# Gate and up products taken for two weight tiles at a time in a decoder layer

## The chip, the cores and the metric

The kernel runs on one core of one Trainium2 chip. The metric is the device time of one execution in microseconds, as the median of several runs. One further execution was recorded by the hardware profiler; the engines are called PE (TensorE, the matmuls), PEld (its weight loads), DVE (VectorE), ACT (ScalarE), POOL (GpSimd) and SP (SyncE, which issues most DMAs).

## What is computed

One layer of a decoder on 256 tokens of 1024 features, in float32: a half feed-forward block, a token mixer, cross-attention to 256 memory tokens, and a second half feed-forward block. The change lies in the two feed-forward blocks:

```python
D_MODEL = 1024
SEQ = 256
D_FF = 2816

def swiglu(h, w_gate, w_up, w_down):
    return (jax.nn.silu(h @ w_gate) * (h @ w_up)) @ w_down

h = rmsnorm(x, ffn1_pre_g[l])
f = swiglu(h, ffn1_w_gate[l], ffn1_w_up[l], ffn1_w_down[l])
x = x + MACARON_WEIGHT * rmsnorm(f, ffn1_post_g[l])
...
h = rmsnorm(x, ffn2_pre_g[l])
f = swiglu(h, ffn2_w_gate[l], ffn2_w_up[l], ffn2_w_down[l])
x = x + MACARON_WEIGHT * rmsnorm(f, ffn2_post_g[l])
```

## The kernel before

**Numbers in two parts.** Matrix products run on operands in the reduced format fp32r. To keep float32's precision each operand is split into a high part (its value in fp32r) and a low part (the rest, in fp32r too), and a product is the sum of low x high, high x high and high x low. ScalarE makes the high part of a weight unit (L76), VectorE the low part (L77). The split of the activations stands in one tile `xs`: for each of the eight 128-feature chunks k, columns 0 to 255 are the high parts of the 256 tokens and columns 256 to 511 the low parts.

**Weights.** All weight tiles of 128 x 128 lie in memory in the order of their use, eight to a unit of 512 KB. `Weights.get` hands out the next tile as a pair (high, low). At the first tile of a unit it has SyncE's loads and the two splits made up to four units ahead; the buffers for high and low parts are six each, so a split waits until the matmuls of an older unit are done.

**Gate and up.** The hidden features are 22 tiles of 128. Features 0 and 1 go through another function (`group`). For each of the features 2 to 21, in each of the two blocks, `gate_up` makes two halves, s = 0 for gate and s = 1 for up. A half takes the eight tiles of one weight unit, k = 0 to 7, into one PSUM tile `ps` of 512 columns (`acc` for gate, `sm` for up in the profile). For every k there are two matmuls with the weights standing still and x moving: the low part of the weights with x's high part, 256 columns, into the right half of `ps` (L574, "short" below), and the high part of the weights with both parts of x, 512 columns, into all of `ps` (L575, "long" below). Each matmul loads its own 128 x 128 weights. At the end of a half ScalarE copies the right half out (L579) and VectorE adds the left half to it (L580). 20 features, 2 halves, 8 tiles and 2 blocks make 640 such pairs of matmuls.

**Around it.** Between the features stand the down products (`row_step`, L298 to L300): 12 matmuls of 512 columns for each feature, here with the activations standing still and the weights moving. Matmuls of 256 columns alone stand in the products of the mixer and the cross-attention (L173 to L175), matmuls of 512 columns alone in L260 to L262 and L298 to L300; the cross-attention's scores (L747 to L749) are twelve of 256 columns between two groups of twelve of 512.

**Order.** TensorE's order is the order in which the program is written, fixed by hand; the orders of the other engines are set by a scheduler, and by hand at the seams between the layer's parts.

Of the kernel before, what the change touches and what calls it, by code (L numbers as in the profile page):

```python
# [17 lines left out]
S = 256  # L18
ND = D // P
# [117 lines left out]
def build(nc, io, tiles_only=False):  # L137
    pr = Program()
    st = {}
# [7 lines left out]
    def tmp(shape, name, **kw):  # L147
        return st["tmp"].tile(shape, F32, name=name, **kw)
# [14 lines left out]
    def defer(run):  # L163
        st["w"].defer(run)
# [22 lines left out]
    def split_plain(X, k, src, eng=nc and nc.vector):  # L187
        nc.scalar.copy(X[:, k, :S], src)
        eng.tensor_tensor(X[:, k, S:], src, X[:, k, :S].bitcast(F32), op=ALU.subtract)
# [29 lines left out]
    def group(name, X, cols, done, before=None, hi_first=False):  # L219

        def run():
            ps = [accum() for _ in range(2)]
            o = [h for p in ps for h in halves(p)]

            def by_lo(ws, k, first):
                for i, (hi, lo) in enumerate(ws):
                    nc.tensor.matmul(o[i], lo, st[X][:, k, :S], start=first and i % 2 == 0,  # L227
                                     stop=k == ND - 1 and hi_first, skip_group_check=True)

            def by_hi(ws, k, first):  # L230
                for i, (hi, lo) in enumerate(ws):
                    nc.tensor.matmul(o[i], hi, st[X][:, k, :S], start=first and i % 2 == 0,  # L232
                                     stop=False, skip_group_check=True)
                    nc.tensor.matmul(o[i], hi, st[X][:, k, S:], start=False,  # L234
                                     stop=k == ND - 1 and not hi_first, skip_group_check=True)
            steps = (by_hi, by_lo) if hi_first else (by_lo, by_hi)
            for k in range(ND):
                if before:
                    before(k)
                ws = [st["w"].get() for _ in cols]  # L240
                for i, by in enumerate(steps):
                    by(ws, k, k == i == 0)
            done(ps)
        names = [name] * len(cols) if isinstance(name, str) else name
        pr.add(run, [(n, k * P, c) for k in range(ND) for n, c in zip(names, cols)])
# [61 lines left out]
    def row_step(X, k, first):  # L307
        w = st["w"].get(UNIT)
        for t in range(2):
            for d in HALVES:  # L310
                row_product(X, st["acc"], k, first, False, t, d, w)
# [47 lines left out]
    def x_spread():  # L359
        pb = rms_spread("x")  # L360
        rB = st["rBx"] = keep([P, S], "rBx")
        nc.scalar.copy(rB, pb[:, :S])
# [198 lines left out]
    def ffn(n, X, before, aside, last):  # L561
        wg, wu, wd = (f"ffn{n}_w_{s}" for s in ("gate", "up", "down"))

        def gate_up(f, done):

            box = []

            def half(s):
                def run():
                    ps = (accum, small)[s]()  # L570
                    for k in range(ND):
                        hi, lo = st["w"].get()
                        x = st[X][:, k, :]
                        nc.tensor.matmul(ps[:, S:], lo, x[:, :S], start=k == 0, stop=False, skip_group_check=True)  # L574
                        nc.tensor.matmul(ps, hi, x, start=False, stop=k == ND - 1, skip_group_check=True)  # L575
                    if s == 0:
                        box.append(st["ffn"].tile([P, 2, S], F32, name="gu", bufs=6))
                    c = tmp([P, S], "cmb")
                    nc.scalar.copy(c, ps[:, S:])  # L579
                    nc.vector.tensor_tensor(box[0][:, s, :], ps[:, :S], c, op=ALU.add)  # L580
                    if s:
                        done(box[0])
                return run
            return [(half(s), [(w, k * P, f * P) for k in range(ND)]) for s, w in enumerate((wg, wu))]

        def finish(f, t):

            src = t
            if f < 2:
                t = st["ffn"].tile([P, 2, S], F32, name="gu", bufs=6)  # L590
                src = src.rearrange("p (i s) -> p i s", i=2)
            nc.vector.tensor_tensor(t, src, st["rBx"][:, None, :].to_broadcast([P, 2, S]), op=ALU.mult)

            def rest():
                nc.scalar.activation(t[:, 0, :], t[:, 0, :], AF.Silu)
                nc.vector.tensor_tensor(t[:, 0, :], t[:, 0, :], t[:, 1, :], op=ALU.mult)
                h = st["h", f] = st["ffn"].tile([P, 1, 2 * S], F32R, name="h", bufs=LAG + 4)
                split_plain(h, 0, t[:, 0, :])
            defer(rest)

        early = []
        first = 2 if n == 1 else 3

        def opened():
            x_spread()
            for f, t in enumerate(early):
                finish(f, t)

        def down(k):
            if k == 0:  # L610
                pr.add(row_acc)
            pr.add(lambda: row_step(st["h", k], 0, k == 0), [(wd, k * P, c * P) for c in range(ND)])

        group([wg, wu] * 2, X, [0, 0, P, P], early.extend, before=before, hi_first=n == 1)
        seam(False)
        for f in range(2, NF):
            gate, up = gate_up(f, early.append if f < first + 1 else lambda t, f=f: finish(f, t))
            pr.add(*gate)
            if f == first:
                side(x_sums if n == 1 else x_root)  # L620
            if f == first + 1:
                side(opened)
            pr.add(*up)
            for run in aside.get(f, ()):
                pr.add(run)
            for k in {2: [], 3: [], 4: [], 5: [0], 6: [1, 2], 7: [3]}.get(f, [f - LAG]):
                down(k)
        down(NF - LATE - 1)
        ks = list(range(NF - LATE, NF))
        side(lambda: st["w"].defer(roots_next))  # L630
        return last(lambda k: st["h", k], ks, [(wd, k * P, c * P) for k in ks for c in range(ND)])
# [163 lines left out]
    def seam(on):  # L795
        pr.add(("seam", on))

    def side(func, *args):
        pr.add(lambda: func(*args))
# [138 lines left out]
    k = K.pop(0)  # L938
# [47 lines left out]
    k = K.pop(0)  # L986
# [141 lines left out]
```

## Time and profile before

| | before |
|---|---|
| median of 3 runs | 578.73 us |
| lowest to highest | 577.92 to 578.73 us |
| the profiled execution, its own time | 580.79 us |
| its span, first to last instruction | 578.6 us |
| PE busy | 565.5 us (98%) |
| PEld busy | 496.7 us (86%) |
| DVE busy | 411.2 us (71%) |
| ACT busy | 341.6 us (59%) |
| the 640 + 640 matmuls of L574 and L575, sum of their shown durations | 410.9 us |

The profile shows one execution. The end of a matmul is modelled and overlaps the next one's start, so the durations of matmuls add up to more than the time they take; the distance between two starts is the better measure. A weight load (PEld) runs beside the matmul ahead of it. The profile's times in order are rounded to 0.01 us, so a step is read over many matmuls, or from several of the same kind.

### The profile page before, as it was taken

How to read it: one execution, taken by the hardware profiler on the slowest of the kernel's cores; microseconds unless marked ns; L12 is line 12 of the kernel's file. 1: busy time of each engine (PE TensorE's matmuls, PEld its weight loads, DVE VectorE, ACT ScalarE, POOL GpSimd, SP SyncE). 2: the span in 40 equal slices, each digit the busy share in tenths (PEclk: the TensorE clock that was granted, in tenths of full speed). 3: DMA queues.
4: the chain of work that ended last, by engine and by line, in shares of the span. 5: the costliest groups of instructions: out<-in, count | busy, mean ns of one | idle time of the engine just before them, and what ended most of it. 6: DMA issues, size and time to landing. Idle time of an engine off the chain costs nothing.

```text
span 578.6 us, 8485 instructions
## 1 busy us (share of the span) xinstructions
PE 565.5 (98%) x3304; PEld 496.7 (86%) x3304; DVE 411.2 (71%) x662; ACT 341.6 (59%) x613; POOL 20.0 (3%) x37
## 2 busy tenths in 40 slices
PE   8799999999999999999999999999999999999995
PEld 8788888888888899988899988879888888888884
DVE  5898666787776678984568676467796766766654
ACT  6588575555555656775359456358674555555543
POOL 0000000000000000450000000001000000000001
PEclk9899999999999999999999999999999999999998
DMA  8885686645646068264256624426655555545202
GB/s 298 310 344 182 254 281 227 217 159 206 204 163 216 18 237 287 79 218 147 72 187 246 219 113 146 146 72 222 253 195 184 202 180 185 200 164 218 74 1 73
DMA packets 29400, 107.04 MB, mean 185 GB/s; under 512 B 2096, under 2 KB 3248, under 8 KB 28976
## 3 DMA queue, kind: packets, MB, share of 16 engines
q1 hardware_dynamic: 28928, 106.14, 52.3%
q8 instruction: 26, 0.43, 0.3%
q10 hardware_dynamic: 432, 0.35, 0.2%
q14 instruction: 14, 0.11, 0.0%
HBM read 105.44 MB, written 1.05 MB: 184 GB/s over the span
## 4 chain that ended last, share of the span: by engine, by line
PE 92%; DVE 3%; DMA 2%; ACT 1%; issue 1%; DVEq 0%; SPq 0%
PE acc L575 13%; PE sm L575 13%; PE acc L298 10%; PE acc L300 9%; PE acc L299 9%; PE acc L574 7%; PE sm L574 7%; PE acc L173 3%; PE acc L174 3%; PE acc L175 3%; PE acc L234 2%; PE acc L232 2%; PE acc L260 2%; PE acc L262 2%; PE acc L261 2%; PE acc L227 2%
## 5 line engine op out<-in xcount | busy, mean ns | idle before, releaser
L77 DVE TENSOR_TENSOR wlo<-wraw,whi 128x1024 fp32r<-128x1024 f32 x183 | 223.7, 1231 | 76.9 <-ACT whi L76 76.4
L76 ACT CAST whi<-wraw 128x1024 fp32r<-128x1024 f32 x184 | 192.5, 1053 | 51.1 <-PE acc L300 41.5
L575 PE MATMUL acc<-xs,whi 128*128 128x512 f32 x320 | 115.9, 401 | 0.0
L575 PE MATMUL sm<-xs,whi 128*128 128x512 f32 x320 | 114.5, 398 | 0.0
L574 PE MATMUL acc<-xs,wlo 128*128 128x256 f32 x320 | 90.4, 282 | 3.1 <-DVE wlo L77 3.1
L574 PE MATMUL sm<-xs,wlo 128*128 128x256 f32 x320 | 90.1, 282 | 0.0
L575 PEld LDWEIGHTS acc<-xs,whi 128*128 128x128 f32 x320 | 60.7, 190 | 14.6
L575 PEld LDWEIGHTS sm<-xs,whi 128*128 128x128 f32 x320 | 60.1, 188 | 14.9
L298 PE MATMUL acc<-whi,h 128*128 128x512 f32 x176 | 69.0, 392 | 0.0
L300 PE MATMUL acc<-whi,h 128*128 128x512 f32 x176 | 68.7, 390 | 0.0
L299 PE MATMUL acc<-wlo,h 128*128 128x512 f32 x176 | 68.5, 389 | 0.0
L574 PEld LDWEIGHTS acc<-xs,wlo 128*128 128x128 f32 x320 | 60.8, 190 | 4.5 <-DVE wlo L77 3.3
L574 PEld LDWEIGHTS sm<-xs,wlo 128*128 128x128 f32 x320 | 60.5, 189 | 0.0
L579 ACT COPY cmb<-acc 128x256 f32<-128x256 f32 x40 | 14.9, 373 | 53.6 <-PE acc L575 53.4
L173 PE MATMUL acc<-xs,wlo 128*128 128x256 f32 x160 | 46.1, 288 | 0.0
L174 PE MATMUL acc<-xs,whi 128*128 128x256 f32 x160 | 45.2, 283 | 0.0
L175 PE MATMUL acc<-xs,whi 128*128 128x256 f32 x160 | 45.2, 283 | 0.0
L579 ACT COPY cmb<-sm 128x256 f32<-128x256 f32 x40 | 14.8, 371 | 50.6 <-PE sm L575 50.6
L300 PEld LDWEIGHTS acc<-whi,h 128*128 128x128 f32 x176 | 33.0, 188 | 7.3
L299 PEld LDWEIGHTS acc<-wlo,h 128*128 128x128 f32 x176 | 33.1, 188 | 7.1
L298 PEld LDWEIGHTS acc<-whi,h 128*128 128x128 f32 x176 | 33.0, 188 | 5.6
L232 PE MATMUL acc<-xs,whi 128*128 128x256 f32 x128 | 32.4, 285 | 0.8 <-ACT whi L108 0.8
(179 smaller groups left out, 896.5 us busy)
## 6 DMA issues: line engine op xcount, KB each, us to landing
wraw<-w SPq DMA_DIRECT2D x91, 1024.0 KB, 4.8
post<-post SPq DMA_DIRECT2D x4, 512.0 KB, 5.2
wraw<-w SPq DMA_DIRECT2D x7, 256.0 KB, 5.8
wraw<-w SPq DMA_DIRECT2D x2, 512.0 KB, 7.2
y<-memt SPq DMA_DIRECT2D x1, 1024.0 KB, 9.9
y<-mem SPq DMA_DIRECT2D x1, 1024.0 KB, 6.9
xt<-xt SPq DMA_DIRECT2D x1, 1024.0 KB, 6.8
out_dram<-y SPq DMA_DIRECT2D x4, 128.0 KB, 1.9
```

Source lines behind the costliest of these rows:

```text
L76: self.nc.scalar.copy(hi, raw)
L77: eng.tensor_tensor(lo, raw, hi.bitcast(F32), op=ALU.subtract)
L173: nc.tensor.matmul(o, lo, X[:, :S], start=first, stop=False, skip_group_check=True)
L174: nc.tensor.matmul(o, hi, X[:, :S], start=False, stop=False, skip_group_check=True)
L175: nc.tensor.matmul(o, hi, X[:, S:], start=False, stop=last, skip_group_check=True)
L232: nc.tensor.matmul(o[i], hi, st[X][:, k, :S], start=first and i % 2 == 0, stop=False, skip_group_check=True)
L298: nc.tensor.matmul(o, a, hi, start=first, stop=False, skip_group_check=True)
L299: nc.tensor.matmul(o, a, lo, start=False, stop=False, skip_group_check=True)
L300: nc.tensor.matmul(o, b, hi, start=False, stop=last, skip_group_check=True)
L574: nc.tensor.matmul(ps[:, S:], lo, x[:, :S], start=k == 0, stop=False, skip_group_check=True)
L575: nc.tensor.matmul(ps, hi, x, start=False, stop=k == ND - 1, skip_group_check=True)
L579: nc.scalar.copy(c, ps[:, S:])
```

## The change

For two weight tiles at a time, the two short matmuls with the low parts come first and then the two long ones with the high parts: low, low, high, high in place of low, high, low, high. Both pairs go into the same PSUM tile as before; the flags that open and close the sum stand on the first short and the last long matmul of the half, as before.

```diff
@@ -568,11 +568,14 @@
             def half(s):
                 def run():
                     ps = (accum, small)[s]()
-                    for k in range(ND):
-                        hi, lo = st["w"].get()
-                        x = st[X][:, k, :]
-                        nc.tensor.matmul(ps[:, S:], lo, x[:, :S], start=k == 0, stop=False, skip_group_check=True)
-                        nc.tensor.matmul(ps, hi, x, start=False, stop=k == ND - 1, skip_group_check=True)
+                    for k in range(0, ND, 2):
+                        ws = [st["w"].get() for _ in range(2)]
+                        for i, (hi, lo) in enumerate(ws):
+                            nc.tensor.matmul(ps[:, S:], lo, st[X][:, k + i, :S], start=k == i == 0, stop=False,
+                                             skip_group_check=True)
+                        for i, (hi, lo) in enumerate(ws):
+                            nc.tensor.matmul(ps, hi, st[X][:, k + i, :], start=False, stop=k + i == ND - 1,
+                                             skip_group_check=True)
```

Only TensorE's order changes. The first place is the start of the first gate half after the features 0 and 1 (the L227 matmuls). A row is line, operation, output <- operands, size and, in brackets, the semaphores of the engines that it waits for; `x2` are two alike, the numbers behind the names tell buffers apart. Before:

```order
L227 MATMUL acc_183<-xs_92,wlo_129 128x256
L227 MATMUL acc_184<-xs_92,wlo_129 128x256 x2
L574 MATMUL acc_302<-xs_92,wlo_186 128x256 [waits DVE_49]
L575 MATMUL acc_302<-xs_92,whi_185 128x512 [waits Activation_49]
L574 MATMUL acc_302<-xs_92,wlo_186 128x256
L575 MATMUL acc_302<-xs_92,whi_185 128x512
```

After, at the same place on TensorE:

```order
L227 MATMUL acc_183<-xs_92,wlo_129 128x256
L227 MATMUL acc_184<-xs_92,wlo_129 128x256 x2
L574 MATMUL acc_302<-xs_92,wlo_186 128x256 [waits DVE_49]
L574 MATMUL acc_302<-xs_92,wlo_186 128x256
L577 MATMUL acc_302<-xs_92,whi_185 128x512 [waits Activation_49]
L577 MATMUL acc_302<-xs_92,whi_185 128x512
L574 MATMUL acc_302<-xs_92,wlo_186 128x256 x2
L577 MATMUL acc_302<-xs_92,whi_185 128x512 x2
```

The second short matmul moved ahead of the first long one, the two waits kept their matmuls, and L575 is now L577. The second place is the end of an up half, where a down product follows. Before:

```order
L574 MATMUL sm_698<-xs_92,wlo_609 128x256
L575 MATMUL sm_698<-xs_92,whi_608 128x512
L298 MATMUL acc_555<-whi_634,h_448 128x512 [waits Activation_49]
L299 MATMUL acc_555<-wlo_635,h_448 128x512 [waits DVE_49]
L300 MATMUL acc_555<-whi_634,h_448 128x512
```

After:

```order
L574 MATMUL sm_698<-xs_92,wlo_609 128x256 x2
L577 MATMUL sm_698<-xs_92,whi_608 128x512 x2
L298 MATMUL acc_555<-whi_634,h_448 128x512 [waits Activation_49]
L299 MATMUL acc_555<-wlo_635,h_448 128x512 [waits DVE_49]
L300 MATMUL acc_555<-whi_634,h_448 128x512
```

The half still ends with a long matmul, and the down product behind it and its waits stayed.

## Rows read from the trace of the kernel before

**Rows 1.** The page: span, and each engine's busy us (share) xinstructions.

```profile
span 578.6 us, 8485 instructions
...
PE 565.5 (98%) x3304; PEld 496.7 (86%) x3304; DVE 411.2 (71%) x662; ACT 341.6 (59%) x613; POOL 20.0 (3%) x37
```

**Rows 2.** The page: the chain that ended last, share of the span by engine.

```profile
PE 92%; DVE 3%; DMA 2%; ACT 1%; issue 1%; DVEq 0%; SPq 0%
```

**Rows 3.** Stretches in both blocks: length, busy us (xinstructions) by engine, clock, DMA, GB/s.

```profile
core 0: us, PE busy (x) PEld busy (x) DVE busy (x) ACT busy (x) POOL busy (x), PEclk, DMA share, GB/s
...
100.00:150.00 50.00, 50.00 (x264) 42.66 (x263) 38.87 (x60) 28.11 (x48) 0.00 (x0) 1.00 0.56 190
...
450.00:500.00 50.00, 50.00 (x264) 42.63 (x264) 34.80 (x48) 26.21 (x42) 0.00 (x0) 1.00 0.54 186
```

**Rows 4.** Waits: who waited for whom, us in total, times, longest.

```profile
DVE wlo L77 <- ACT whi L76: 76.4, 106, 3.2
...
ACT whi L76 <- PE acc L300: 41.5, 43, 2.6
...
PE acc L574 <- DVE wlo L77: 3.1, 1, 3.1
```

**Rows 5.** The page's groups: gate and up matmuls, busy us, mean ns, idle before.

```profile
L575 PE MATMUL acc<-xs,whi 128*128 128x512 f32 x320 | 115.9, 401 | 0.0
L575 PE MATMUL sm<-xs,whi 128*128 128x512 f32 x320 | 114.5, 398 | 0.0
L574 PE MATMUL acc<-xs,wlo 128*128 128x256 f32 x320 | 90.4, 282 | 3.1 <-DVE wlo L77 3.1
L574 PE MATMUL sm<-xs,wlo 128*128 128x256 f32 x320 | 90.1, 282 | 0.0
```

**Rows 6.** Order of time on PE, one gate and up half: start us, us, instruction.

```profile
110.90 0.28 PE L574 MATMUL acc<-xs,wlo 128*128 128x256 f32 x1
111.02 0.40 PE L575 MATMUL acc<-xs,whi 128*128 128x512 f32 x1
111.25 0.28 PE L574 MATMUL acc<-xs,wlo 128*128 128x256 f32 x1
...
116.55 0.40 PE L298 MATMUL acc<-whi,h 128*128 128x512 f32 x1
```

**Rows 7.** The same in a stream of short ones alone, 104 steps apart.

```profile
309.83 0.28 PE L173 MATMUL acc<-xs,wlo 128*128 128x256 f32 x1
...
322.31 0.28 PE L175 MATMUL acc<-xs,whi 128*128 128x256 f32 x1
```

**Rows 8.** The same in a stream of long ones alone, 45 steps apart.

```profile
272.59 0.39 PE L298 MATMUL acc<-whi,xs 128*128 128x512 f32 x1
...
282.79 0.39 PE L298 MATMUL acc<-whi,xs 128*128 128x512 f32 x1
```

**Rows 9.** The same, twelve short and twelve long ones in turn.

```profile
330.58 0.28 PE L747 MATMUL xsc<-xk,xs 128*128 128x256 f32 x1
...
334.76 0.28 PE L747 MATMUL xsc<-xk,xs 128*128 128x256 f32 x1
...
334.99 0.28 PE L749 MATMUL xsc<-xk,xs 128*128 128x256 f32 x1
...
336.19 0.40 PE L260 MATMUL acc<-whi,xs 128*128 128x512 f32 x1
336.42 0.40 PE L261 MATMUL acc<-wlo,xs 128*128 128x512 f32 x1
336.66 0.39 PE L262 MATMUL acc<-whi,xs 128*128 128x512 f32 x1
...
337.35 0.39 PE L262 MATMUL acc<-whi,xs 128*128 128x512 f32 x1
...
338.94 0.28 PE L747 MATMUL xsc<-xk,xs 128*128 128x256 f32 x1
```

**Rows 10.** Weight loads (PEld) among the short ones: start us, us, instruction.

```profile
334.88 0.19 PEld L749 LDWEIGHTS xsc<-xk,xs 128*128 128x128 f32 x1
334.99 0.19 PEld L747 LDWEIGHTS xsc<-xk,xs 128*128 128x128 f32 x1
335.11 0.19 PEld L748 LDWEIGHTS xsc<-xk,xs 128*128 128x128 f32 x1
```

## The prediction

> **What bounds the kernel now.** I read the page first, then the waits, then TensorE's own order of time. TensorE (PE) is busy for 565.5 of the 578.6 us [rows 1] and holds 92% of the chain that ended last [rows 2]. In the stretches of the two feed-forward blocks it is busy for every microsecond of the stretch, at a granted clock of 1.00, while VectorE (DVE), ScalarE (ACT) and the DMA engines have a fifth or more of the time left [rows 3]. Who waits for whom agrees: ScalarE's splitting of weights (L76) waits for the down products' matmuls (L300) to give a buffer back, VectorE's (L77) waits for ScalarE, and of the 640 + 640 gate and up matmuls one alone waited for VectorE, 3.1 us at the start [rows 4]. So in the stretch that the change touches the weights are ready before they are needed, and the time between two matmul starts on TensorE is the time of the kernel.
>
> How long a matmul takes has to be read from start to start. The durations in the groups, 282 ns for a short matmul (256 columns) and 398 to 401 ns for a long one (512) [rows 5], overlap their neighbours: over one gate and one up half, 16 short and 16 long ones take from 110.90 to 116.55 us, 5.65 us [rows 6]. A pair of short and long is 0.353 us, and the four matmuls of two weight tiles, which I call a block, 0.706 us. There are 640 pairs (320 + 320 of each line [rows 5]), so 320 blocks and 226 us, 39% of the span.
>
> **The change part by part.** It adds, removes and resizes nothing: the same 1,280 matmuls, each with its own weight load. The orders of VectorE, ScalarE, GpSimd and SyncE stay as they are, DMA issues included. Three things move.
>
> *The waits.* The first short matmul of a half carries the wait for the low parts, the first long one that for the high parts. Both tiles of a block lie in one weight unit of eight, which both orders take at the half's first step; the first long one now comes one short matmul later. VectorE's low part is made after ScalarE's high part, so no wait is added or longer. The 3.1 us wait stands before the first short matmul in both orders. Cost: nothing, covered by weights that are ready; without that cover it would still be the same wait.
>
> *The buffers and the evacuation.* The last matmul of a half is long in both orders, so ScalarE's copy (L579) and the return of the high part's buffer come at the same place; the low part's buffer comes back one long matmul earlier, which nobody uses, since the next split starts with the high part. Cost nothing.
>
> *The changes between short and long.* Here the time is made. A stream of short matmuls alone runs at 12.48 us for 104 of them, 0.120 us each [rows 7]; a settled stream of long ones at 10.20 us for 45, 0.2267 us each [rows 8]. Two of each would be 0.693 us. The alternating block takes 0.706, so it loses 0.013 us, 0.0065 for each return from short to long. All of this loss is 320 x 0.013 = 4.2 us; no more than that can be gained by order. The block of the change has one return in place of two, but more matmuls in a row of each kind, and how the loss depends on that must be read elsewhere in the kernel. The attention scores alternate twelve short ones (L747 to L749) with twelve long ones. From 330.58 to 338.94 us there are two such rounds, 8.36 us, against 24 x (0.120 + 0.2267) = 8.32: a long round loses 0.020 us, not 0.0065 [rows 9]. Nothing is lost among the short ones: the first two take 0.23 us in place of 0.24 (334.76 to 334.99). The first five long ones take 1.16 in place of 1.133 (336.19 to 337.35), and the first two 0.47 in place of 0.453 (to 336.66) [rows 9]. So a return to long ones has a price of at most 0.020 us, paid over three to five long ones; in the alternation three pairs pay 3 x 0.0065, the same 0.020.
>
> That gives three readings for the new block of two short and two long:
> 1. The rows behind a switch put together: 0.23 + 0.47 = 0.70 us against 0.706, a gain of 0.0063. Times 320: 2.0 us.
> 2. One price of 0.020 in as many blocks as it takes to pay it. Paid over four long ones, that is two blocks: 0.010 a block in place of 0.013, a gain of 0.003, times 320: 1.0 us. Over three long ones it is no gain, over five 0.008 a block and a gain of 1.6 us.
> 3. The whole price in every block: 0.020 in place of 0.013, a loss of 0.007, times 320: 2.1 us slower.
>
> The first two rest on rows of short runs, the third asks that two long ones pay what five pay in the rows. I take the middle of the first two, 1.5 us, and keep 0 to 2.0 as the ends of this case. The profiled execution took 580.79 us, its span 578.6 and 2.2 around it; less 1.5 that is 579.3. It stands 2.06 above the median of the runs, 578.73, so the forecast for the median is 577.2 us. All of the gain passes to the end, as no other engine holds TensorE in these stretches; their shares in [rows 3] rise by 1.5 in 226 us, under one per cent.
>
> A rule of the Trainium skill speaks against any effect. The rows show 0.120 and 0.2267 us for a matmul with its own load [rows 7, 8], and 0.353 for a mixed pair [rows 6]. In "TensorE: Matmul & The Clock Gate", section "Back-to-back issue gap", the distance between starts at full clock is the columns over 2.4 GHz plus about 2.5 ns, 109 and 216 ns here, whatever came before. By that a block would take 0.650 us in either order, and the sum would be zero. The trace does not agree, neither in the size of the steps nor in that a pair is more than its two parts.
>
> **The rivals.** *Order does not count.* The loss of a pair may belong to these operands and not to alternation: no row of this kernel has two long matmuls in a row with x as the moving operand and weights loaded, so the 0.2267 of rows 8 is a neighbour's figure. Then nothing moves: 578.7 us. For it: the first row after the switch is no longer than a long one in the alternation, and the price per long one, 0.0065, fits both the alternation and the first three behind a switch. Against: one short matmul or twelve, the return costs alike, so it looks like a price of switching. By the skill's rule above the result would be this one as well.
>
> *Slower: the full price in every block.* With two short ones in a row TensorE may fall back wholly into the pace of a short stream, as the scores do (0.119 to 0.120 from the second one on), and the two long ones then pay the whole 0.020. It decides from the point where a block costs more than 0.706 us. Price 2.1 us: 580.8. Against it: by the rows the second long one ends with 0.017 of the delay taken and 0.010 of it was advance from the first two short ones.
>
> A variant, that the load of the second low tile, 0.19 us long, isn't hidden behind a short matmul, would cost up to 320 x 0.07 = 22 us, but in the scores such loads start 0.12 us apart and hold nobody up [rows 10]; I give it no chance worth a number.
>
> *The loss goes wholly.* If only a single long one between short ones loses, a block comes down to 0.693: 320 x 0.013 = 4.2 us, 574.6 us. Against it: the long rounds lose too [rows 9].
>
> **How the numbers follow.** Forecast case, grouping recovers 0 to 2.0 us, most likely 1.5: 0.57. Order does not count: 0.26. Full price: 0.11. Loss gone: 0.06. A measurement of this kernel can tell about 0.2%, 1.16 us, from no change. Of the forecast case some four fifths, 0.45, lie beyond that; with 0.06 that makes 0.51 for faster. The rest of it, 0.12, and 0.26 make 0.38 for the same; 0.11 for slower. For the range I leave out the loss gone and the full price, 0.17 together: from 578.73 - 2.0, less half of the spread of the runs shown (0.81), 576.3, up to no change plus that half, 579.1.
>
> **What would show it.** In the profile after, starts of TensorE over one gate and up half: 16 pairs in about 5.61 us (0.701 a block) if right, 5.65 if order does not count, 5.70 with the full price, 5.55 with the loss gone. The two long starts of a block should stand 0.23 and 0.24 apart, the two short ones 0.11 to 0.12. VectorE's 3.1 us wait and the order of everything else should be as before, and the down products' 0.2267 unchanged. Wrong would be: a wait on L574 beside the one at the start, or a gain that stands in another line than the gate and up matmuls.

## The result and the profile after

| | before | after |
|---|---|---|
| median of 9 runs | 580.55 us | 575.69 us |
| lowest to highest | 577.92 to 581.13 us | 575.42 to 577.63 us |
| span of the profiled execution | 578.6 us | 573.6 us |

The ratio is 0.9928, with a 95% interval of 0.9911 to 0.9945: the change makes the kernel faster, by about 0.7% in this comparison. Some executions of either kernel hold one stretch of a few microseconds near 22 us at the low clock and are some 1.6 us longer for it; by their times they were more frequent on the before side here (six of nine runs at 580.37 us or more; two of nine after, at 576.83 and 577.63), and like against like the difference is 3.2 us, 0.56% (shown below).

The page of the kernel after, answering [rows 1, 5]: span, busy us by engine, and the gate and up matmuls (L575 is now L577).

```profile
span 573.6 us, 8485 instructions
...
PE 562.7 (98%) x3304; PEld 496.4 (87%) x3304; DVE 411.1 (72%) x662; ACT 341.6 (60%) x613; POOL 19.9 (3%) x37
...
L577 PE MATMUL acc<-xs,whi 128*128 128x512 f32 x320 | 100.5, 395 | 0.0
L577 PE MATMUL sm<-xs,whi 128*128 128x512 f32 x320 | 100.5, 395 | 0.0
...
L574 PE MATMUL sm<-xs,wlo 128*128 128x256 f32 x320 | 63.1, 279 | 0.0
L574 PE MATMUL acc<-xs,wlo 128*128 128x256 f32 x320 | 62.9, 278 | 0.0
```

The other engines do the same work in the same time. The mean duration of long matmuls went from 398 to 401 ns down to 395, of short ones from 282 to 278 and 279. (The summed busy time, 100.5 us, is less than 320 x 395 ns: matmuls of one line that overlap are counted once, and more of them stand in a row now. So the 410.9 us of the table of before is such a busy time too, and no sum of durations: 320 x 401 ns alone would be 128 us, not 115.9. The means and the starts count.) What a block costs is read from the starts, answering [rows 6]: start us, us, instruction on PE; `x2` are two matmuls.

```profile
116.84 0.40 PE L574 MATMUL acc<-xs,wlo 128*128 128x256 f32 x2
117.07 0.63 PE L577 MATMUL acc<-xs,whi 128*128 128x512 f32 x2
117.54 0.39 PE L574 MATMUL acc<-xs,wlo 128*128 128x256 f32 x2
117.77 0.63 PE L577 MATMUL acc<-xs,whi 128*128 128x512 f32 x2
118.23 0.40 PE L574 MATMUL acc<-xs,wlo 128*128 128x256 f32 x2
...
122.41 0.39 PE L298 MATMUL acc<-whi,h 128*128 128x512 f32 x1
...
125.13 0.40 PE L574 MATMUL acc<-xs,wlo 128*128 128x256 f32 x2
```

Gate and up, 16 pairs, take 122.41 - 116.84 = 5.57 us in place of 5.65. The blocks alternate: 0.70 us for the first, 0.69 for the second, so the second loses nothing against 0.693. The down product behind them takes 125.13 - 122.41 = 2.72 us; before, the same 12 matmuls took 2.74, from the row below to the first row of [rows 6]:

```profile
108.16 0.40 PE L298 MATMUL acc<-whi,h 128*128 128x512 f32 x1
```

A feature is 8.29 us in place of 8.39. Over fourteen features in a row, from 440.98 to 558.40 us before and from 437.26 to 553.36 us after (starts of L298), the difference is 0.094 us a feature. Of the 40 features 32 stand in one piece ahead of a down product: 32 x 0.094 = 3.0 us. The other eight stand in longer stretches at the start of each block: they gain 0.3 us in the second block and lose 0.1 in the first. Together that is 3.2 us, about 2.6 of it in the pairs and 0.7 in the down products, each rounded.

Two stretches near 22 us make up most of the rest of the 5.0 us between the two profiles. Length, busy us (xinstructions) by engine, granted clock, DMA; first the kernel before:

```profile
22.00:24.00 2.00, 2.00 (x9) 1.72 (x9) 2.00 (x2) 0.00 (x0) 0.00 (x0) 0.61 0.79 283
24.00:26.00 2.00, 2.00 (x11) 1.81 (x10) 0.66 (x2) 0.37 (x1) 0.00 (x0) 0.54 0.92 377
```

The kernel after:

```profile
22.00:24.00 2.00, 2.00 (x15) 1.73 (x13) 2.00 (x2) 0.07 (x1) 0.00 (x0) 1.00 0.77 279
24.00:26.00 2.00, 2.00 (x15) 1.84 (x15) 0.74 (x3) 1.53 (x4) 0.00 (x0) 1.00 0.99 373
```

The clock was at 0.61 and 0.54 in the one and at 1.00 in the other. Whether that is part of the change was the first question for the chip.

### The profile page after: what moved, and what is told of

The parts are those of the page before. It is cut to its first block, busy times and chain, and to the rows that moved or that the text cites. A ratio compares the mean times of both kernels' runs of the same rounds, so it can differ in the third digit from the quotient of the medians.

```text
span 573.6 us, 8485 instructions
## 1 busy us (share of the span) xinstructions
PE 562.7 (98%) x3304; PEld 496.4 (87%) x3304; DVE 411.1 (72%) x662; ACT 341.6 (60%) x613; POOL 19.9 (3%) x37
## 4 chain that ended last, share of the span: by engine, by line
PE 94%; DVE 3%; DMA 1%; issue 1%; ACT 0%; DVEq 0%; SPq 0%
PE acc L577 13%; PE sm L577 13%; PE acc L298 10%; PE acc L299 9%; PE acc L300 9%; PE sm L574 6%; PE acc L574 6%; PE acc L234 3%; PE acc L232 3%; PE acc L173 3%; PE acc L227 3%; PE acc L174 3%; PE acc L175 3%; PE acc L262 2%; PE acc L261 2%; PE acc L260 2%
## 5 line engine op out<-in xcount | busy, mean ns | idle before, releaser
L577 PE MATMUL acc<-xs,whi 128*128 128x512 f32 x320 | 100.5, 395 | 0.0
L577 PE MATMUL sm<-xs,whi 128*128 128x512 f32 x320 | 100.5, 395 | 0.0
L298 PE MATMUL acc<-whi,h 128*128 128x512 f32 x176 | 68.6, 390 | 0.0
L574 PE MATMUL sm<-xs,wlo 128*128 128x256 f32 x320 | 63.1, 279 | 0.0
L574 PE MATMUL acc<-xs,wlo 128*128 128x256 f32 x320 | 62.9, 278 | 0.0
L577 PEld LDWEIGHTS acc<-xs,whi 128*128 128x128 f32 x320 | 48.7, 189 | 0.0
L577 PEld LDWEIGHTS sm<-xs,whi 128*128 128x128 f32 x320 | 48.7, 189 | 0.0
L173 PE MATMUL acc<-xs,wlo 128*128 128x256 f32 x160 | 46.1, 288 | 0.0
L174 PE MATMUL acc<-xs,whi 128*128 128x256 f32 x160 | 45.2, 283 | 0.0
L175 PE MATMUL acc<-xs,whi 128*128 128x256 f32 x160 | 45.2, 283 | 0.0
L298 PEld LDWEIGHTS acc<-whi,h 128*128 128x128 f32 x176 | 33.1, 188 | 7.0
L232 PE MATMUL acc<-xs,whi 128*128 128x256 f32 x128 | 34.0, 295 | 1.7 <-ACT whi L108 1.7
```

The costliest lines, as they stand in the source:

```text
L173: nc.tensor.matmul(o, lo, X[:, :S], start=first, stop=False, skip_group_check=True)
L174: nc.tensor.matmul(o, hi, X[:, :S], start=False, stop=False, skip_group_check=True)
L175: nc.tensor.matmul(o, hi, X[:, S:], start=False, stop=last, skip_group_check=True)
L298: nc.tensor.matmul(o, a, hi, start=first, stop=False, skip_group_check=True)
L574: nc.tensor.matmul(ps[:, S:], lo, st[X][:, k + i, :S], start=k == i == 0, stop=False, skip_group_check=True)
L577: nc.tensor.matmul(ps, hi, st[X][:, k + i, :], start=False, stop=k + i == ND - 1, skip_group_check=True)
```

## Experiments

All compare with the kernel before on the same chip, or read the steps of 16 pairs (gate and up of one feature, start of the first to start of the down product) from the trace, which no clock of another stretch disturbs.

**1. The kernel before, again.** No edit.

> The kernel before, unchanged. The profile after is 5.0 us shorter in span, of which the gate and up products (16 pairs of matmuls in 5.57 us in place of 5.65, forty times) give 3.2 us; the other 1.7 us stand near 22 us, where the trace of before shows a granted clock of 0.61 and 0.54 (22 to 26 us) and that of after 1.00. Theory A: that low clock is a matter of chance, of when the clock rises at the start, and not of the change; then the runs of this kernel fall into two groups about 1.6 us apart, the shorter one with a mean granted clock of 0.996 to 0.997, the longer with 0.994. Rival B: it belongs to the order low, high, low, high; then all its runs have 0.994 and lie together, and the ratio to the kernel before is 1.000 with no spread of 1.6 us.

Measured: ratio 1.0005 (0.9994 to 1.0016). Twelve runs in two groups: eight from 578.26 to 579.24 us at a mean granted clock of 0.996 to 0.999, four from 580.38 to 580.52 at 0.993 to 0.994. The order is the same in all of them, so rival B is out: the low clock comes and goes with one and the same kernel. The profiled execution has it:

```profile
20.00:22.00 2.00, 1.32 (x5) 1.15 (x6) 2.00 (x3) 0.03 (x1) 0.00 (x0) 0.77 0.35 86
22.00:24.00 2.00, 2.00 (x9) 1.71 (x8) 2.00 (x2) 0.00 (x0) 0.00 (x0) 0.50 0.86 313
```

**2. The kernel after, again.** No edit.

> The kernel after, unchanged, beside the kernel before on one chip, each run with its granted clock. The kernel before, run again, fell into two groups, 578.2 to 579.4 us at a mean clock of 0.995 to 0.999 and 580.0 to 580.5 at 0.993 to 0.994. Theory A (the order gives the 73 ns that 16 pairs are shorter, forty times, 2.9 us, and the clock near 22 us is chance): the runs at 0.995 or more lie 2.9 us below those of before at the same clock, 575.4 to 576.4, those at 0.994 at 576.8 to 577.7, and the ratio is 0.995. Rival B (the new order itself avoids the low clock): hardly a run of it lies at 0.994, while the kernel before has a quarter of its runs there, and the ratio is 0.994 or less.

Measured: ratio 0.9934 (0.9915 to 0.9953), six runs: five from 575.20 to 575.49 us at a clock of 0.996 to 0.999, one of 577.11 at 0.994. Beside them the kernel before had six runs from 578.28 to 579.12 at 0.996 to 0.999 and five from 580.00 to 580.67 at 0.994. At the same clock the change gives 578.58 - 575.34 = 3.2 us between the medians of the upper groups, and 3.4 between the lower. That is theory A, with a little more than its 2.9, though not by its sum: the pairs give about 2.6, and the 0.02 us of each down product, which it left out, give 0.7. The ratio came out below 0.995 because five of eleven against one of six happened to lie in the low group. Over both sets the kernel after had 3 of 15 runs at 0.994 and the kernel before, in this set and the one of experiment 1, 16 of 51; I can't tell these shares apart, so rival B has no support.

**3. Four tiles together.**

```diff
-                    for k in range(0, ND, 2):
-                        ws = [st["w"].get() for _ in range(2)]
+                    for k in range(0, ND, 4):
+                        ws = [st["w"].get() for _ in range(4)]
```

> Four weight tiles together: four short matmuls, then four long ones. In the profile after, a block of two loses 0.0033 us against streams of one size (0.697 and 0.6933), the alternation 0.0065 per pair. Theory A (a price for each return to long matmuls, whatever the run's length up to here): half the returns of the kernel after, 0.0033 each; 16 pairs in 5.56 us, kernel 0.5 us faster than the kernel after, 3.7 us faster than before at the same clock. Theory B (the price of a return grows with the run of long ones up to the 0.020 us of the scores' rounds): 0.010 to 0.017 per return; 16 pairs in 5.59 to 5.61 us, 0.5 to 1.7 us slower than the kernel after.

Measured: ratio 0.9984 (0.9974 to 0.9994). On PE:

```profile
92.24 0.64 PE L574 MATMUL acc<-xs,wlo 128*128 128x256 f32 x4
...
97.85 0.39 PE L298 MATMUL acc<-whi,h 128*128 128x512 f32 x1
...
100.60 0.64 PE L574 MATMUL acc<-xs,wlo 128*128 128x256 f32 x4
```

16 pairs in 5.61 us: theory B. Half as many returns from short to long as after the change, and 0.04 us more for a feature's gate and up. The down product takes 2.75 us here, as before the change (2.74) and not 2.72.

**4. All eight together.**

```diff
-                    for k in range(0, ND, 2):
-                        ws = [st["w"].get() for _ in range(2)]
+                    for k in range(0, ND, 8):
+                        ws = [st["w"].get() for _ in range(8)]
```

> All eight low parts of a half, then all eight high parts. Theory A (a price of 0.0033 per return): 16 pairs in 5.55 us, 0.8 us faster than the kernel after. Theory B (a full round costs 0.020 us as in the scores): 16 pairs in 5.547 + 2 x 0.020 = 5.587 us, 0.5 us slower than the kernel after, still 2.7 us faster than before at the same clock.

Measured: ratio 0.9963 (0.9952 to 0.9975).

```profile
92.12 1.11 PE L574 MATMUL acc<-xs,wlo 128*128 128x256 f32 x8
...
97.71 0.39 PE L298 MATMUL acc<-whi,h 128*128 128x512 f32 x1
```

16 pairs in 5.59 us, as theory B had it (5.587): a return after a full run costs the 0.020 us that the scores' rounds showed [rows 9].

**5. Alternating, but not the same tile.** To the kernel before:

```diff
+                    ws = [st["w"].get() for _ in range(ND)]
...
+                    for k in range(ND):
+                        by_lo(k)
+                        by_hi((k + 4) % ND, k == ND - 1)
```

Here `by_lo` and `by_hi` are the short and the long matmul of before, with the weights `ws[k]`.

> Short and long matmuls alternate as before, but the long one belongs to the tile four further on, so no two matmuls in a row share a chunk of x or a weight tile. Theory A (the alternation of sizes is what costs): 16 pairs in 5.65 us as before. Rival B (it is that a short and a long one in a row read the same chunk of x): 16 pairs in 5.55 to 5.58 us, as with the change or better.

Measured (one run, 578.58 us; the kernel before beside it 578.88):

```profile
91.90 0.28 PE L574 MATMUL acc<-xs,wlo 128*128 128x256 f32 x1
...
97.55 0.40 PE L298 MATMUL acc<-whi,h 128*128 128x512 f32 x1
```

5.65 us. That neighbours share x's chunk or a weight unit's tile plays no part.

**6. The other half of the PSUM tile.** To the kernel before:

```diff
-                        nc.tensor.matmul(ps[:, S:], lo, x[:, :S], start=k == 0, stop=False, skip_group_check=True)
+                        nc.tensor.matmul(ps[:, :S], lo, x[:, :S], start=k == 0, stop=False, skip_group_check=True)
```

> Order as before, but the short matmul adds into the left half of the PSUM tile in place of the right one, so that it no longer begins on the columns that the long one has written last. Theory A (sizes alternate, nothing else counts): 16 pairs in 5.65 us as before. Rival B (the price is one of writing the same PSUM columns too soon after): other steps in the rows, and 16 pairs in 5.55 to 5.60 us or, if the long one now begins too soon on the short one's columns, over 5.66.

Measured (one run, 579.03 us; before 579.12):

```profile
92.40 0.28 PE L574 MATMUL acc<-xs,wlo 128*128 128x256 f32 x1
...
98.05 0.40 PE L298 MATMUL acc<-whi,h 128*128 128x512 f32 x1
```

5.65 us again: not a matter of which columns were written last.

**7 and 8. All of one size.** The long matmul in two, in the order of before (7) and in that of after (8). The edit to the kernel before; the one to the kernel after cuts its long matmul in the same way:

```diff
-                        nc.tensor.matmul(ps, hi, x, start=False, stop=k == ND - 1, skip_group_check=True)
+                        for i in range(2):
+                            h = slice(i * S, (i + 1) * S)
+                            nc.tensor.matmul(ps[:, h], hi, x[:, h], start=False, stop=k == ND - 1 and i == 1,
+                                             skip_group_check=True)
```

> Every long matmul is cut into two of 256 columns, each with its own weight load; order low, high, high per tile, no sizes to alternate. Theory A (a price for changes of size): 48 matmuls in 48 x 0.120 = 5.76 us for 16 tiles, the same with both orders, 4.5 us in all slower than before. Rival B (a price for going from low to high parts and back): 5.76 plus 16 x 0.0065 = 5.86 us.

> The same cut into 256 columns, in the order of the change: low, low, then four high ones. Theory A: 5.76 us for 16 tiles, the order changes nothing where all are of one size. Rival B: shorter than the alternating one by 0.07 us, as the change was.

Measured, one run each: 583.65 and 583.17 us. First the alternating, then the grouped one:

```profile
136.00 0.28 PE L574 MATMUL acc<-xs,wlo 128*128 128x256 f32 x1
...
141.75 0.40 PE L298 MATMUL acc<-whi,h 128*128 128x512 f32 x1
```

```profile
135.54 0.40 PE L574 MATMUL acc<-xs,wlo 128*128 128x256 f32 x2
...
141.30 0.40 PE L298 MATMUL acc<-whi,h 128*128 128x512 f32 x1
```

5.75 and 5.76 us: with one size the order changes nothing. So the price needs matmuls of two sizes, as theory A says.

**9. High parts first.** To the kernel after: the two loops of a block change places, and the opening and closing flags with them.

```diff
                         for i, (hi, lo) in enumerate(ws):
-                            nc.tensor.matmul(ps[:, S:], lo, st[X][:, k + i, :S], start=k == i == 0, stop=False,
+                            nc.tensor.matmul(ps, hi, st[X][:, k + i, :], start=k == i == 0, stop=False,
                                              skip_group_check=True)
                         for i, (hi, lo) in enumerate(ws):
-                            nc.tensor.matmul(ps, hi, st[X][:, k + i, :], start=False, stop=k + i == ND - 1,
+                            nc.tensor.matmul(ps[:, S:], lo, st[X][:, k + i, :S], start=False, stop=k + i == ND - 1,
                                              skip_group_check=True)
```

> Two tiles together as in the kernel after, but high, high, low, low. The number of returns from short to long is the same, the last one of a half moves into the following half or down product. Theory A (the price belongs to the run lengths of two and two): a feature, 16 pairs and 12 down matmuls, takes 8.29 us as in the kernel after (before 8.387). Rival B (low parts first is what helps): 8.34 us or more. The first long matmul no longer waits for VectorE's low part near 20.9 us, which can save up to 0.5 us once.

Measured: ratio 0.993 (0.9916 to 0.9943), median 574.89 us. A feature takes 8.29 us, as in the kernel after:

```profile
133.35 0.62 PE L574 MATMUL acc<-xs,whi 128*128 128x512 f32 x2
...
141.64 0.62 PE L574 MATMUL acc<-xs,whi 128*128 128x512 f32 x2
```

Theory A. Which of the two comes first is nothing; the first long matmuls of the first feature do start earlier, which may be the half microsecond between the medians, but the intervals overlap.

**10. Groups of three, three and two.**

```diff
-                    for k in range(0, ND, 2):
-                        ws = [st["w"].get() for _ in range(2)]
+                    for k, n in ((0, 3), (3, 3), (6, 2)):
+                        ws = [st["w"].get() for _ in range(n)]
```

> Groups of three, three and two tiles. Measured price of one return from short to long: 0.0062 us with runs of one, 0.0033 with two, 0.0153 with four, 0.020 with eight. Theory A (the price grows with the run beyond two): about 0.009 for three; 16 pairs in 5.547 + 4 x 0.009 + 2 x 0.0033 = 5.59 us. Rival B (runs of two are no special place, and three lies at 0.0033 or less as well): 5.56 to 5.57 us.

Measured, one run, 575.86 us:

```profile
132.92 0.52 PE L574 MATMUL acc<-xs,wlo 128*128 128x256 f32 x3
...
138.51 0.39 PE L298 MATMUL acc<-whi,h 128*128 128x512 f32 x1
```

5.59 us: theory A. With 16 x (0.120 + 0.2267) = 5.547 us as the time without any loss, the rows give:

| tiles in a group | 16 pairs, us | returns in them | us lost per return |
|---|---|---|---|
| 1 (before) | 5.65 | 16 | 0.0064 |
| 2 (after) | 5.57 | 8 | 0.003 |
| 3, 3, 2 | 5.59 | 6 | 0.007 |
| 4 | 5.61 | 4 | 0.016 |
| 8 | 5.59 | 2 | 0.02 |

The starts are rounded to 0.01 us, so the last column is good to 0.001 us at its top and to 0.005 at its bottom.

**11. VectorE's second sum later.** To the kernel after: the second of the two sums of squares at the start is put off until the next unit's split is made.

```diff
-            nc.vector.tensor_reduce(st["xsq"][:, i, :], x.rearrange("p c s -> p s c"), axis=AX.X, op=ALU.add)
+            def total(i=i, x=x):
+                nc.vector.tensor_reduce(st["xsq"][:, i, :], x.rearrange("p c s -> p s c"), axis=AX.X, op=ALU.add)
+            if i == 0:
+                total()
+            else:
+                defer(total)
```

> The kernel after, and VectorE's second sum of squares (1.97 us) behind the first split of the features' weights in place of ahead of it. Where the clock rises early, TensorE waits 3.1 us for that split and a stretch of 3.4 us at the low clock follows, which costs 1.6 us. Theory A (the wait brings the low clock): the split is ready some 2 us earlier, the wait shrinks to about 1 us, no run lies at 0.994, and the runs at an early clock are up to 2 us faster than the fastest of the kernel after, 573.5 to 575.5 us; where the clock rises late nothing is gained. Rival B (the low clock has another cause): a fifth to a third of the runs stay at 0.994 and 1.6 us above the others.

Measured: ratio 0.9911 (0.9897 to 0.9924), median 573.67 us; five runs from 573.52 to 574.37, all at a clock of 0.997 or more. VectorE's order of time:

```profile
16.93 0.34 DVE L506 TENSOR_SCALAR half<-gain 128x1 f32<-128x1 f32 x4
17.18 1.22 DVE L77 TENSOR_TENSOR wlo<-wraw,whi 128x1024 fp32r<-128x1024 f32 x1
18.31 2.06 DVE L500 TENSOR_REDUCE q<-y 128x256 f32<-128x1024 f32 x1
```

The split is done at 18.4 us, and the wait that the kernel before shows at 20.9 us [rows 4] is gone. That gains more than I had thought where the clock rises late: this execution is one of those (its 256-column matmuls start 0.21 us apart until 9.1 us), and its span is 571.5 us, 1.6 under that of the kernel after run again.

**12. Both.** The edits of 9 and 11 together.

> High, high, low, low together with VectorE's second sum of squares behind the first split. Of the profiles so far the two with a wait of 3.1 us before the first feature's low part have a stretch at the low clock, the eleven with 2.4 us or less have none. Theory A (the wait brings it): no run at 0.994 or less, all within about 1 us, 573.0 to 574.2 us. Rival B (the low clock has another cause): about a quarter of the runs lie 1.6 us above the others at 0.994.

Measured: ratio 0.9898 (0.9877 to 0.9918), median 573.96 us, five runs from 573.04 to 574.43, all at 0.998. All ten runs of it and of experiment 11, 574.43 us at most, lie under the lowest of the fifteen of the kernel after, 575.20, with the kernel before at 577.9 to 578.4 us at its lowest beside each of these sets; the intervals of the ratios overlap a little. Between the two there is no difference that I can tell. Of ten runs without the wait none had the low clock. By the kernel before's 16 of 51 that would be luck of 2%, by the kernel after's 3 of 15 of 11%, so theory A is likely, not proved. Nor is the low clock all that lengthens a run: of the nine runs of the kernel before in this set three, from 579.67 to 581.13 us, had 0.996 to 0.997. In the profiles the stretch came with a wait of 3.1 us (the two of the kernel before) and never with 2.4 us or less (twelve others, this one's among them), as here in the kernel after run again, whose clock stayed up:

```profile
PE acc L574 <- DVE wlo L77: 2.4, 1, 2.4
```

## Why the prediction was right in direction and too small

**What bounds the kernel.** Right. TensorE stayed the bound, nothing else moved, and what the matmuls' starts gave came out at the end.

**Waits, buffers, evacuation at no cost.** Right: the orders of the other engines are those of before, and in the profile after not even the 3.1 us wait is there, because its clock rose late and TensorE came late to the place.

**The changes between short and long.** The kind of effect was right, and experiments 5 to 8 show it: the sizes count, not the operands, the columns or which part is low. That the sizes change is needed for the loss, but does not always bring it (see what stays open). The size of the gain was wrong: forecast 1.5 us in 320 blocks, 0.0047 us a block, at most 0.0063; the rows give (5.65 - 5.57) / 8, about 0.009. Of 16 pairs I expected 5.61 us, the rows say 5.57; 577.2 us was forecast, 575.69 measured, 0.6 below the range. Three things were missed.

*The step that failed is the use of rows from long runs for short ones.* Reading 1 put the rows just behind a switch of the scores together, 0.70 us a block; that is what the first block of two shows. The second takes 0.69: it loses nothing, which no row of the scores can show, since there two long ones are followed by ten more. Reading 2, a price of 0.020 us handed out over the long ones and so a loss of 0.008 to 0.013 in a block, is refuted by the table above: a block of two loses 0.003. The price of a return does not simply grow with how many long ones follow, as it falls from runs of one to runs of two and then rises to the 0.020 us of full runs. Reading 3, the full price in every block, is what runs of eight cost, and with runs of four most of it; the slower rival named a real mechanism, one that begins at longer runs than two.

*The term that was not in the sum* is the down product. It follows an alternation in the kernel before and pays 0.02 us for that in its first matmuls. With 33 places that is 0.7 us. The prediction had the down products unchanged, and named a gain in another line than the gate and up matmuls as a sign of being wrong; this is one.

*The comparison held the clock's chance.* About 1 us of the 4.2 that the ratio stands for is the share of runs with the low clock. That bears on the ratio alone: from 577.2 to 575.69 us, both without that stretch, the miss of 1.5 us is about what the first two make (2.6 in place of 1.5 us in the pairs, and 0.7).

**The loss goes wholly,** the rival that I gave 0.06, came nearest: 574.6 us. But the loss did not go wholly: of its 4.2 us about 2.6 were won, and the other 0.7 came from the down products, which that sum did not hold, so the nearness of the time is in part luck. My reason against it, that long rounds lose too, was the same wrong step.

**Order does not count** is refuted by experiments 3, 4 and 10. The rule of the Trainium skill, "TensorE: Matmul & The Clock Gate", section "Back-to-back issue gap", gives 0.650 us for a block in any order; the rows give 0.706, 0.70 and 0.69 for the orders tried here. The section calls this the gap of an isolated matmul, which the prediction left out; what it gives for a stream with weight loads, about 131 ns for 512 columns, no row here shows either (0.2267 us). For matmuls of one size (experiments 7 and 8) order does not count, but the step is 0.120 us and not the rule's 0.109.

**What stays open.** What the state is that a change of size disturbs is not settled. One more finding speaks against a fixed price per return. In the trace of the kernel before, ahead of the first down product, the alternation ran without any loss:

```profile
33.07 0.28 PE L574 MATMUL sm<-xs,wlo 128*128 128x256 f32 x1
...
46.25 0.40 PE L298 MATMUL acc<-whi,h 128*128 128x512 f32 x1
```

38 pairs in 13.18 us, 0.347 each, the sum of the two streams. The trace held these rows, and I read only the later ones [rows 6]. In the kernel after the same 38 pairs take 13.24 us, so there the change loses:

```profile
31.35 0.39 PE L574 MATMUL sm<-xs,wlo 128*128 128x256 f32 x2
...
44.59 0.39 PE L298 MATMUL acc<-whi,h 128*128 128x512 f32 x1
```

So the same order can run at 0.347 or at 0.353 us a pair, by the state in which it is entered, and keeps to it. What sets the state the rows do not say. The second block of the kernel before begins with the same alternation:

```profile
398.44 0.28 PE L574 MATMUL acc<-xs,wlo 128*128 128x256 f32 x1
...
412.58 0.61 PE L286 MATMUL pb<-const,rcx 128*128 128x128 f32 x4
...
413.73 0.28 PE L574 MATMUL sm<-xs,wlo 128*128 128x256 f32 x1
...
421.51 0.39 PE L298 MATMUL acc<-whi,h 128*128 128x512 f32 x1
```

Here 40 pairs take 14.14 us, 0.3535 each, with no down product ahead of them in the block, so the down product alone is not what brings the loss. Four small matmuls (L286) stand at 31.92 us, shortly ahead of the 38 pairs without loss, and again at 412.58 us, where the 22 pairs from 413.73 us on lose as much as ever (7.78 us, 0.354 each). So small matmuls ahead do not by themselves bring the better state.

## What to carry to other kernels

Where matmuls of two sizes share a bound TensorE, the order of sizes is worth one to two per cent of their time, but not by a rule of "fewer changes": here groups of two were best, and groups of four gained half as much in the pairs and nothing in the down products. Read the price of a pattern from rows of that very pattern, in every place where it occurs, and count what the pattern does to the matmuls that follow it; a price taken from longer runs gave half of the gain. And before a difference of half a per cent is put down to an edit, look at the granted clock of both profiles in stretches of a few microseconds.

## What the runs showed of the hardware that I had not expected

- A short and a long matmul in turn cost 0.347 or 0.353 us with the same operands, and the better state lasted over 38 pairs until the first down product; the second block was in the worse one from its start.
- A return from short to long matmuls costs 0.0064, 0.003, 0.016 and 0.02 us with runs of one, two, four and eight, where the alternation is in its worse state.
- At the start the clock rises at different times in executions of the same instructions. In the kernel after's profile the 256-column matmuls start 0.21 us apart until 12.8 us and 0.12 from there on. The profile's column of the granted clock reads 1.00 on both sides of this, so the rise is read from the steps alone. It cost little, a span of 573.6 us against 573.1 for the kernel after run again, whose steps grew short some 6 us sooner, since TensorE came to the next weights just when they were ready:

```profile
12.35 0.41 PE L232 MATMUL acc<-xs,whi 128*128 128x256 f32 x1
12.56 0.38 PE L234 MATMUL acc<-xs,whi 128*128 128x256 f32 x1
12.77 0.29 PE L232 MATMUL acc<-xs,whi 128*128 128x256 f32 x1
12.90 0.28 PE L234 MATMUL acc<-xs,whi 128*128 128x256 f32 x1
```

An early rise left a wait of 2.2 to 3.1 us. The two waits of 3.1 us were each followed by a stretch at the low level, 1.2 GHz: there the quick start was the slower one (spans of 578.6 and 578.3 us). The two of 2.2 and 2.4 us (experiments 5 and 2) were not, and their spans, 576.4 and 573.1 us, lie half a microsecond under those of late rises with the same steps (576.9 in experiment 6, 573.6 in the kernel after).
